# A queue of deferred work gets borders: the steps of a layer norm's chain dealt one to a pair of weight blocks, and no flush before the pointwise product

## The chip, the cores and the metric

The kernel runs on one core of one Trainium2 chip. TensorE (PE in the profile) multiplies matrices, VectorE (DVE) and ScalarE (ACT) work on tiles in the on-chip memory, GpSimd (POOL) takes a few small steps, and SyncE (SP) issues nearly all transfers. Each engine works through its own list of instructions in a fixed order and waits for the others by semaphores. The metric is the device time of one execution in microseconds (us); less is better.

## The reference, cut to what matters

One layer of a streaming encoder on a sequence of 256 rows and a width of 4096, all in float32:

```python
xn = rms_norm(h, norm_in_g[i])
proj = xn @ w_in[i]                       # 4096 x 14336
q, k, v, z_a, a_c, g_c, z_c = jnp.split(proj, ...)          # seven times 2048 columns
y_a = rms_norm(chunked_attention(q, k, v, rel_table[i]), attn_out_g[i]) * jax.nn.silu(z_a)
# the convolution module, 2048 channels
u = a_c * jax.nn.sigmoid(g_c)
u = causal_depthwise_conv(u, w_dw) + b_dw                    # 31 taps
u = jax.nn.silu(layer_norm(u, ln_g, ln_b))
y_c = rms_norm(u @ w_pw + b_pw, conv_out_g[i]) * jax.nn.silu(z_c)
h = h + jnp.concatenate([y_a, y_c], axis=-1) @ w_out[i]
gate = jax.nn.sigmoid(rms_norm(h, ple_norm_g[i]) @ w_ple_gate[i] + b_ple_gate[i])
h = h + gate * (p[i] @ w_ple[i])
return rms_norm(h, final_g)
```

## The kernel before, in words

Every large product takes its operands as a rounded high part and the rest as a low part, and adds three products: high by high, low by high, high by low. So each weight block that a transfer brings (`wt`, 128 rows by 2 x 512 columns) is split on the spot: ScalarE casts it to `wh` (L218), VectorE subtracts to get `wl` (L219), and TensorE reads both (L386). The tiles `wh` and `wl` have three buffers each, so a cast waits until TensorE has done with the block three before.

`mixed_product` makes two output groups of 512 columns at once. It goes through 16 "pairs" of weight blocks in an order written by hand (`early` and `valued`, for instance). A plain pair is two blocks of 12 products each. A pair with a star is a "seven": it is done with 21 products in place of 24, for which VectorE must add up weights first (`ua`, `ub`, L442 to L447) and both engines must split four tiles. At the last seven `on_helpers` collects the sums of the helper banks (`acc_P..`) into the tiles `z`; after the last pair the results in the banks `acc` are added to `z` (L510).

Work that is not urgent waits in a queue, `later`: a list of small functions. After each pair, `deal(n)` calls `fill(n)`, which pops n functions and so writes their instructions into the program at that place, behind that pair's weight cast (`behind_casts`); it then writes one step of the attention from a second list, `heads`. The numbers n stand in tables, one for each pair: `early_fills`, or a tuple at the call. A scheduler then fixes the order on each engine; the place at which a function is written says where it may stand at the earliest, more than where it will stand.

The change concerns two such products that follow each other, and what comes after. The first (`q, vs[2] = blocks(...)`, order `early`) makes the fourth group of queries and the third of values; here the last 56 taps of the convolution are dealt out and the layer norm begins. The second (`k, vs[3] = blocks(...)`, order `valued`) makes the last keys and values; here the rest of the layer norm is dealt out. Then the pointwise product with `w_pw` begins, which reads the layer norm's result as the tiles `uS` (named `big_t`).

The layer norm works on four tiles `cv` of 128 x 1024, one for 512 channels. Its chain is: `total` (sums over the tiles), `fold`, `mean` (a product on TensorE), then `center` 16 times (L766) and `square` 4 times (L770, L774), `fold`, `variance` (two small products L780, then a power on GpSimd, tile `r_ln`), `diagonals` (two VectorE steps, L789), `spread` (products L798, then ScalarE writes `rs`, L749), then `swish` 16 times (a multiply by `rs` on VectorE, L803, and Silu on ScalarE, L804, behind a table load), and `split` 16 times (a cast on ScalarE, L814, and a subtraction on VectorE, L815, into `uS`). Between the steps of the chain stand empty functions, `rest`, four at a time, which use up places of the tables. What is left in the queue when the two products end is written at once by `fill(len(later))` ahead of the pointwise product: 20 functions, four `swish` and 16 `split`.

`late_pool`, called at the last seven of the second product, closes a pool and opens another, `more`, in which `uS` lies; no `split` can be written earlier.

Of the kernel before, what the change touches and what calls it, by code (L numbers as in the profile page):

```python
# [17 lines left out]
NB = 512  # L18
# [7 lines left out]
def hybrid_block(  # L26
# [24 lines left out]
    _, T, D = x.shape  # L51
# [34 lines left out]
    def tmp_psum():  # L86
        return ps_tmp.tile([P, 512], F32, tag="tmp", name="tmp_ps")
# [6 lines left out]
    o_q, o_k, o_v, o_za = 0, AW, 2 * AW, 3 * AW  # L94
# [41 lines left out]
    def rsqrt(dst, src, n):  # L136

        nc.vector.tensor_scalar(dst, src, 1.0 / n, EPS, ALU.mult, ALU.add)
        nc.gpsimd.tensor_tensor(dst, dst, mhalf[:, : dst.shape[1]], ALU.pow)
# [9 lines left out]
    def big_tile(pool=None):  # L149
        return (pool or big).tile([P, 4, 2, T], F32R, tag="big", name="big_t")  # L150
# [29 lines left out]
    later = deque()  # L180
# [3 lines left out]
    def behind_casts():  # L184
        return tc.issue_after(last_cast[0].ins) if last_cast else nullcontext()

    def fill(n):
        with behind_casts():
            for _ in range(min(n, len(later))):
                later.popleft()()  # L190

    heads = deque()
# [1 line left out]
    def deal(n):  # L194
        fill(n)
        if heads:
            with behind_casts():
                heads.popleft()()
# [129 lines left out]
    def units(text):  # L328

        return [(int(u.rstrip("*")), u.endswith("*")) for u in text.split()]  # L330
# [4 lines left out]
    early = units("1 3 5 7 0* 9 2* 11 4* 13 6* 15 8 10 12 14")  # L335

    valued = units("1 3 5 7 8 0* 9 2* 10 4* 11 6* 12 13 14 15")

    early_fills = (4, 6, 7, 1, 5, 1, 5, 1, 5, 1, 2, 4, 6, 6, 6, 4)
# [149 lines left out]
    def sum_tiles(**kw):  # L489

        kw = kw or dict(tag="stage")
        t = [spool.tile([P, NH, NB], F32, name="z", **kw) for _ in range(2)]
        return t, [[t[j][:, h] for j in range(2)] for h in range(NH)]

    def scaled_pair(w, col, apart, order, r, fills, home={}, then=lambda: None, **kw):

        t, z = [], []

        def on_helpers(helper):
            for dst, src in zip((t, z), sum_tiles(**home)):  # L500
                dst.extend(src)
            then()
            nc.scalar.activation(z[0][0], helper["P1"], AF.Identity, scale=r[:, :1])
            helper_sums(helper, z)
            for h, j in QUARTERS[1:]:
                nc.scalar.activation(z[h][j], z[h][j], AF.Identity, scale=r[:, h : h + 1])

        c = mixed_product(w, col, xT, xS, order, on_helpers, fills=fills, apart=apart, **kw)
        for h, j in QUARTERS:
            stt(  # L510
                z[h][j], c[h][j], r[:, h : h + 1], z[h][j],
                ALU.mult, ALU.subtract if j else ALU.add,
            )
        return t
# [222 lines left out]
    def layer_norm_swish():  # L737

        add = nc.vector.tensor_tensor
        st = {}  # L740

        def fold(s):
            add(s[:, :2, :], s[:, :2, :], s[:, 2:, :], ALU.add)
            add(s[:, 0, :], s[:, 0, :], s[:, 1, :], ALU.add)
            return s[:, 0, :]

        def stat(key, m, scale=1.0):
            st[key] = cpool.tile([P, T], F32, tag="ln_stat", name=key)
            nc.scalar.activation(st[key], m, AF.Identity, scale=scale)  # L749

        def mean(s):

            m = tmp_psum()
            nc.tensor.matmul(m[:, :T], mean_w, s, start=True, stop=True)
            stat("mu", m[:, :T])

        def total(c):
            if c == 0:
                st["s"] = hd_tile("lnsum")
                add(st["s"], conv[0], conv[1], ALU.add)  # L760
            elif c > 1:
                add(st["s"], st["s"], conv[c], ALU.add)

        def center(c, i):
            cv = conv[c]
            nc.vector.tensor_tensor(cv[:, i, :], cv[:, i, :], st["mu"], ALU.subtract)  # L766

        def square(c):
            s = hd_tile("sq")
            nc.scalar.activation(s, conv[c], AF.Square)  # L770
            if c == 0:
                st["q"] = s
            else:
                add(st["q"], st["q"], s, ALU.add)  # L774

        def variance(s):

            m = tmp_psum()
            for h in range(NH):
                nc.tensor.matmul(  # L780
                    m[:, h : h + 1], s[:, h * P : (h + 1) * P], mean_w[:, :1],
                    start=True, stop=True,
                )
            st["r"] = cpool.tile([P, NH], F32, name="r_ln")
            rsqrt(st["r"], m[:, :NH], 1)

        def diagonals(s):
            for h in range(NH):
                nc.vector.tensor_scalar(  # L789
                    s[:, h * P : (h + 1) * P], ident, st["r"][:, h : h + 1], None, ALU.mult  # L790
                )

        def spread(s):

            m = tmp_psum()
            for h in range(NH):
                d = s[:, h * P : (h + 1) * P]
                nc.tensor.matmul(m[:, h * P : (h + 1) * P], mean_w, d, start=True, stop=True)  # L798
            stat("rs", m[:, :T], float(CW))

        def swish(c, i):
            cv, b = conv[c], 4 * c + i
            nc.vector.tensor_tensor(cv[:, i, :], cv[:, i, :], st["rs"], ALU.mult)  # L803
            nc.scalar.activation(  # L804
                cv[:, i, :], cv[:, i, :], AF.Silu,
                scale=ln_g[:, b : b + 1], bias=ln_b[:, b : b + 1],
            )

        def split(c, i):
            if i == 0:  # L810
                assert more is not None
                uS.append(big_tile(more))
            hi, lo = uS[c][:, i, 0, :], uS[c][:, i, 1, :]
            nc.scalar.copy(hi, conv[c][:, i, :])  # L814
            nc.vector.tensor_tensor(lo, conv[c][:, i, :], hi.bitcast(F32), ALU.subtract)  # L815

        n = len(conv)
        rest = [lambda: None] * 4
        later.extend(partial(total, c) for c in range(n))
        later.append(lambda: fold(st["s"]))  # L820
        later.extend(rest)
        later.append(lambda: mean(st["s"][:, 0, :]))
        later.extend(rest)
        for c in range(n):
            later.extend(partial(center, c, i) for i in range(4))
            later.append(partial(square, c))
        later.append(lambda: fold(st["q"]))
        later.extend(rest)
        later.append(lambda: variance(st["q"][:, 0, :]))
        later.extend(rest)  # L830
        later.append(lambda: diagonals(st["s"][:, 0, :]))
        later.extend(rest)
        later.append(lambda: spread(st["s"][:, 0, :]))
        later.extend(rest)
        for c in range(n):
            later.extend(partial(swish, c, i) for i in range(4))
        for c in range(n):
            later.extend(partial(split, c, i) for i in range(4))
# [84 lines left out]
    qs, ks, vs, biases = {}, {}, {}, {}  # L923

    def hd_tile(name):
        return spool.tile([P, GH, T], F32, tag="hd", name=name, bufs=5)

    def load_bias(g):
        bias = biases[g] = hd_tile("bias")
        span = 2 * MAXR + 1  # L930
        nc.sync.dma_start(
            bias,
            bass.AP(
                tensor=rel_table.tensor,
                offset=rel_table.offset + g * GH * span + MAXR + P - (T - 1),
                ap=[[1, P], [span, GH], [1, T]],
            ),
        )
        nc.gpsimd.memset(bias[: P // 2, :, : P // 2], NEG)

    def queries(g, q):
        qs[g] = act.tile([P, GH, T], F32, tag="act", name="qT")
        to_heads(q, qs[g])
# [5 lines left out]
    def blocks(cols, order, fills, **kw):  # L949
        return scaled_pair(w_in0, cols[0], cols[1] - cols[0], order, r_x, fills, **kw)  # L950
# [9 lines left out]
    def late_pool():  # L960
# [18 lines left out]
    keys(2, early_fills)  # L979
    layer_norm_swish()  # L980
    load_bias(2)
    q, vs[2] = blocks((o_q + 3 * NB, o_v + 2 * NB), early, (4,))
    queries(3, q)
    attention(2)
    k, vs[3] = blocks(
        (o_k + 3 * NB, o_v + 3 * NB), valued, (5, 5, 4, 5, 4, 2, 3, 2, 3, 2, 3, 4, 4, 4, 4, 4),
        then=late_pool,
    )
    keyed(3, k)
# [8 lines left out]
        )  # L998
        return t

    fill(len(later))

    point = units("0 1 2 3 4 5 6 7")
    y_c = []
# [175 lines left out]
    _, z = sum_tiles()  # L1180
# [60 lines left out]
    def sum_of(h, at):  # L1241
        s = end[:, 0, h : h + 1]
        pin(nc.vector.tensor_reduce(s, ssq_f[:, h, :at], AX.X, ALU.add))
        return s
# [45 lines left out]
    s = sum_of(1, n_f + 1)  # L1290
# [35 lines left out]
```

## Time and profile before

| | us |
|---|---|
| median of three timed runs | 2039.97 |
| the three runs | 2035.58, 2039.97, 2040.53 |
| the profiled execution | 2035.71 |
| its span, from the first to the last instruction | 2033.9 |
| TensorE busy in the span | 2015.2 |
| VectorE busy | 1912.3 |
| ScalarE busy | 1184.6 |
| TensorE's mean granted clock, share of full | 0.998 |

The four executions known fall in two pairs, 2035.6 and 2035.7, 2040.0 and 2040.5; their mean is 2037.9. The profiled one belongs to the lower pair. A busy share of an engine is the time in which one of its instructions ran, over the span; TensorE's products overlap each other, so the pace at which they start says more about it than how long one takes.

### The profile page before, as it was taken

To read this page: it belongs to the slowest core of one execution; us is meant where nothing else is said; L and a number is where in the kernel's file an instruction comes from. 1 tells how busy PE (TensorE), PEld (TensorE's weight loads), DVE (VectorE), ACT (ScalarE), POOL (GpSimd) and SP (SyncE) were. 2 spreads that over 40 slices of the span, in tenths; PEclk is the share of its full clock that TensorE was granted. 3 is DMA by queue.
4 is the path that set the end of the run, shared out by engine and by line. 5 is a ranking of instruction groups with operands and counts; after the bars stand their busy time and mean duration, and the time that the engine had idled before them with its cause. 6 is when DMAs were issued, how large, how long until landed. Compare 5 with 4: busy or idle time off the path is not lost.

```text
span 2033.9 us, 25980 instructions
## 1 busy us (share of the span) xinstructions
PE 2015.2 (99%) x9094; PEld 1661.5 (82%) x9094; DVE 1912.3 (94%) x2728; ACT 1184.6 (58%) x1530; POOL 7.7 (0%) x19
## 2 busy tenths in 40 slices
PE   9999999999999999999999999999999999999997
PEld 7888888888888888878888888888888888888876
DVE  7999999989999998986899999999999999999998
ACT  7655545555455544675566566676565666665555
POOL 0000000000000000000000000000000000000000
PEclk9999999999999999999999999999999999999999
DMA  8666666566665666555666666676666656666765
GB/s 288 194 196 203 202 196 197 176 196 192 205 205 166 196 199 195 175 186 186 190 217 202 197 210 210 220 232 206 208 199 212 209 187 207 199 223 204 234 208 179
DMA packets 157756, 412.28 MB, mean 203 GB/s; under 512 B 12974, under 2 KB 16190, under 8 KB 157626
## 3 DMA queue, kind: packets, MB, share of 16 engines
q1 hardware_dynamic: 156976, 409.80, 63.4%
q8 instruction: 71, 1.16, 0.2%
q10 hardware_dynamic: 650, 0.84, 0.1%
q14 instruction: 59, 0.48, 0.1%
HBM read 406.39 MB, written 4.19 MB: 202 GB/s over the span
## 4 chain that ended last, share of the span: by engine, by line
PE 53%; DVE 1%; issue 1%; ACT 0%; DMA 0%; POOLq 0%; POOL 0%; ACTq 0%; DVEq 0%
PE acc L386 40%; PE acc_P L386 12%; PE acc L233 1%; PE tmp_ps L170 1%; DVE wl L219 0%; DMA wt<-in_w_ple_dram 0%; DMA wt<-in_w_in_dram 0%; DVE big_t L815 0%; ACT wh L218 0%; ACT uh L218 0%; DVE ul L219 0%; ACT hc L1256 0%; DVE z L1196 0%; PE tmp_ps L891 0%; DVE z L1232 0%
## 5 line engine op out<-in xcount | busy, mean ns | idle before, releaser
L386 PE MATMUL acc<-wh,big_t 128*128 128x512 f32 x4252 | 1312.3, 391 | 0.8 <-DVE wh L577 0.5
L218 ACT CAST wh<-wt 128x1024 fp32r<-128x1024 f32 (+1 forms) x737 | 712.8, 978 | 562.0 <-PE acc L386 409.9
L386 PEld LDWEIGHTS acc<-wh,big_t 128*128 128x128 f32 x4252 | 795.4, 188 | 166.8 <-ACT big_t L156 1.3
L219 DVE TENSOR_TENSOR wl<-wt,wh 128x1024 fp32r<-128x1024 f32 (+1 forms) x737 | 823.6, 1130 | 49.8 <-ACT wh L218 46.7
L386 PE MATMUL acc<-wl,big_t 128*128 128x512 f32 x2126 | 819.7, 391 | 2.3 <-DVE wl L219 2.1
L386 PEld LDWEIGHTS acc<-wl,big_t 128*128 128x128 f32 x2126 | 398.8, 188 | 87.5 <-DVE wl L219 4.5
L696 DVE SCALAR_TENSOR_TENSOR cv<-uT,dw,cv 128x249 f32<-128x249 f32 (+22 forms) x480 | 209.4, 467 | 0.6
L218 ACT CAST uh<-ub 128x1024 fp32r<-128x1024 f32 x126 | 132.5, 1051 | 119.1 <-DVE ub L447 100.9
L218 ACT CAST uh<-ua 128x1024 fp32r<-128x1024 f32 x126 | 132.7, 1053 | 84.3 <-DVE ua L443 78.8
L386 PE MATMUL acc_P<-uh,big_t 128*128 128x512 f32 x528 | 161.9, 392 | 0.0
L219 DVE TENSOR_TENSOR ul<-ub,uh 128x1024 fp32r<-128x1024 f32 x126 | 153.9, 1221 | 7.3 <-ACT uh L218 6.7
L219 DVE TENSOR_TENSOR ul<-ua,uh 128x1024 fp32r<-128x1024 f32 x126 | 153.9, 1221 | 0.4 <-ACT uh L218 0.2
L386 PEld LDWEIGHTS acc_P<-uh,big_t 128*128 128x128 f32 x528 | 98.0, 188 | 23.0 <-ACT uh L218 3.5
L442 DVE TENSOR_TENSOR ua<-wt 128x512 f32<-128x512 f32 x126 | 86.7, 688 | 23.1 <-DMA wt<-in_w_in_dram 14.6
L386 PE MATMUL acc_P<-ul,big_t 128*128 128x512 f32 x264 | 101.6, 393 | 0.0
L443 DVE TENSOR_TENSOR ua<-wt 128x512 f32<-128x512 f32 x126 | 86.5, 686 | 1.9 <-DMA wt<-in_w_in_dram 1.8
L447 DVE TENSOR_TENSOR ub<-ub,wt 128x512 f32<-128x512 f32 x126 | 86.6, 687 | 0.6
L446 DVE TENSOR_TENSOR ub<-ua,wt 128x512 f32<-128x512 f32 x126 | 86.5, 687 | 0.3
L386 PE MATMUL acc_P<-wh,big_t 128*128 128x512 f32 x252 | 78.0, 390 | 0.0
L386 PE MATMUL acc<-uh,big_t 128*128 128x512 f32 x252 | 78.0, 390 | 0.0
L386 PE MATMUL acc_P<-uh,comb_t 128*128 128x512 f32 x228 | 70.3, 391 | 0.1
L386 PEld LDWEIGHTS acc_P<-ul,big_t 128*128 128x128 f32 x264 | 49.4, 188 | 13.1 <-DVE ul L219 2.8
(212 smaller groups left out, 1310.3 us busy)
## 6 DMA issues: line engine op xcount, KB each, us to landing
wt<-in_w_in_dram SPq DMA_DIRECT2D x447, 512.0 KB, 4.1
wt<-in_w_out_dram SPq DMA_DIRECT2D x128, 512.0 KB, 4.2
wt<-in_w_ple_gate_dram SPq DMA_DIRECT2D x128, 512.0 KB, 4.1
wt<-in_w_pw_dram SPq DMA_DIRECT2D x32, 512.0 KB, 4.7
hc<-in_x_dram SPq DMA_DIRECT2D x8, 512.0 KB, 5.8
wt<-in_w_ple_dram SPq DMA_DIRECT2D x8, 512.0 KB, 4.4
xin<-in_x_dram SPq DMA_DIRECT2D x7, 512.0 KB, 7.9
out_dram<-hc SPq DMA_DIRECT2D x12, 256.0 KB, 2.5
```

The lines of the kernel that those rows point to most:

```text
L170: nc.tensor.transpose(pt[:, i * T + h * P : i * T + (h + 1) * P], src[:, h, b] if len(src.shape) == 4 else src[:, h, b * P : (b + 1) * P], ...
L218: nc.scalar.copy(wh[:, :kc, :], wt[:, :kc, :]),
L219: nc.vector.tensor_tensor(wl[:, :kc, :], wt[:, :kc, :], wh[:, :kc, :].bitcast(F32), ALU.subtract),
L233: nc.tensor.matmul(acc, a, b[:, k, :], start=kb == 0 and kind == 0, stop=kb == kblocks - 1 and kind == 2,)
L386: nc.tensor.matmul(banks[name], a, b, start=name not in begun, stop=final and ends[name] == n and kind == 2 and not (left and name in "P2 ...
L442: plus(ua[:, 0], w0[:, 0], w0[:, 1])
L443: plus(ua[:, 1], w0[:, 1], w1[:, 1])
L446: plus(ub[:, 0], ua[:, 0], w1[:, 1])
L447: plus(ub[:, 1], ub[:, 0], w1[:, 0])
L696: nc.vector.scalar_tensor_tensor(cv[:, i, PAD - k :], uT[:, i, : T + k - PAD], dw[:, b, k : k + 1], cv[:, i, PAD - k :], ALU.mult, ALU.add,)
```

## The change

A border, `None`, may stand in the queue. `fill` stops at a border, and the next `fill` of at least one removes it and goes on. The empty functions are gone; a border stands behind each of the six chain steps `fold`, `mean`, `fold`, `variance`, `diagonals` and `spread`, so that two of these steps are never written after the same pair. The first product takes the table `early_fills` in place of four functions after each pair, the second has a new table, and the queue is empty when the second product ends, so the flush is replaced by an assertion.

```diff
     def fill(n):
+
         with behind_casts():
-            for _ in range(min(n, len(later))):
+            if n and later and later[0] is None:
+                later.popleft()
+            for _ in range(n):
+                if not later or later[0] is None:
+                    break
                 later.popleft()()
...
-        rest = [lambda: None] * 4
         later.extend(partial(total, c) for c in range(n))
-        later.append(lambda: fold(st["s"]))
-        later.extend(rest)
-        later.append(lambda: mean(st["s"][:, 0, :]))
-        later.extend(rest)
+        later.extend((lambda: fold(st["s"]), None, lambda: mean(st["s"][:, 0, :]), None))
         for c in range(n):
             later.extend(partial(center, c, i) for i in range(4))
             later.append(partial(square, c))
-        later.append(lambda: fold(st["q"]))
-        later.extend(rest)
-        later.append(lambda: variance(st["q"][:, 0, :]))
-        later.extend(rest)
-        later.append(lambda: diagonals(st["s"][:, 0, :]))
-        later.extend(rest)
-        later.append(lambda: spread(st["s"][:, 0, :]))
-        later.extend(rest)
+        later.extend((lambda: fold(st["q"]), None, lambda: variance(st["q"][:, 0, :]), None))
+        later.extend((lambda: diagonals(st["s"][:, 0, :]), None, lambda: spread(st["s"][:, 0, :]), None))
...
-    q, vs[2] = blocks((o_q + 3 * NB, o_v + 2 * NB), early, (4,))
+    q, vs[2] = blocks((o_q + 3 * NB, o_v + 2 * NB), early, early_fills)
...
-        (o_k + 3 * NB, o_v + 3 * NB), valued, (5, 5, 4, 5, 4, 2, 3, 2, 3, 2, 3, 4, 4, 4, 4, 4),
+        (o_k + 3 * NB, o_v + 3 * NB), valued, (1, 5, 5, 5, 6, 1, 1, 1, 6, 3, 7, 3, 5, 5, 3, 0),
...
-    fill(len(later))
+    assert not later
```

By these tables, in the second product, `swish` is now written after the 9th to 11th pair, where it was after the 14th to 16th and in the flush, and `split` after the 12th to 15th pair, where all of it was in the flush.

What the scheduler makes of it is seen in three places. The names are those of the text above; line numbers behind the queue's function are five higher in the kernel after the change. In the second product, ScalarE, from the scaling factor `rs` on, before:

```order
L749 ACTIVATE rs<-tmp_ps 128x256
L506 ACTIVATE z<-z,r_x 128x512
L218 CAST wh<-wt 128x1024
L506 ACTIVATE z<-z,r_x 128x512 x2
L804 ACT_TABLE_LOAD
L804 ACTIVATE cv<-cv,prm 128x256 x4
L218 CAST wh<-wt 128x1024 x2
L804 ACTIVATE cv<-cv,prm 128x256 x4
L218 CAST wh<-wt 128x1024 x2
L804 ACTIVATE cv<-cv,prm 128x256 x8
L814 CAST big_t<-cv 128x256 x16
L218 CAST wh<-wt 128x1024 x4
```

The same stretch of ScalarE after the change:

```order
L754 ACTIVATE rs<-tmp_ps 128x256
L223 CAST wh<-wt 128x1024
L809 ACT_TABLE_LOAD
L809 ACTIVATE cv<-cv,prm 128x256 x16
L511 ACTIVATE z<-z,r_x 128x512 x3
L819 CAST big_t<-cv 128x256 x8
L223 CAST wh<-wt 128x1024
L819 CAST big_t<-cv 128x256 x5
L223 CAST wh<-wt 128x1024 x2
L819 CAST big_t<-cv 128x256 x3
L223 CAST wh<-wt 128x1024 x7
```

The weight casts that stood between the Silus now stand behind all of them: 16 Silus, the three scalings of `z` and eight casts of `split` follow each other with no `wh` between, while the run of `split` casts ahead of the pointwise product's first weights is gone.

At the border between the second product and the pointwise product, TensorE before (`kT` are the keys, `tmp_ps` the scores, `wh_7929` and `wl_7930` the pointwise product's first weights):

```order
L851 MATMUL tmp_ps_7868<-ident_103,z_7666 128x128 x4
L868 MATMUL tmp_ps_7961<-kT_7861,qT_7024 128x128
L869 MATMUL tmp_ps_7961<-kT_7861,qT_7024 128x256
L386 MATMUL acc00_7921<-wh_7929,big_t_7882 128x512 x2
L386 MATMUL acc10_7923<-wh_7929,big_t_7882 128x512 x2
L386 MATMUL acc01_7922<-wh_7929,big_t_7882 128x512 x2
L386 MATMUL acc11_7924<-wh_7929,big_t_7882 128x512 x2
L868 MATMUL tmp_ps_7973<-kT_7861,qT_7024 128x128
L869 MATMUL tmp_ps_7973<-kT_7861,qT_7024 128x256
L386 MATMUL acc00_7921<-wl_7930,big_t_7882 128x512
```

TensorE at the same border after the change:

```order
L846 MATMUL tmp_ps_7912<-ident_103,z_7703 128x128 x4
L391 MATMUL acc00_7921<-wh_7929,big_t_7721 128x512 x2
L391 MATMUL acc00_7921<-wl_7930,big_t_7721 128x512
L391 MATMUL acc10_7923<-wh_7929,big_t_7721 128x512 x2
L391 MATMUL acc10_7923<-wl_7930,big_t_7721 128x512
L391 MATMUL acc01_7922<-wh_7929,big_t_7721 128x512 x2
L391 MATMUL acc01_7922<-wl_7930,big_t_7721 128x512
L391 MATMUL acc11_7924<-wh_7929,big_t_7721 128x512 x2
L391 MATMUL acc11_7924<-wl_7930,big_t_7721 128x512
L391 MATMUL acc00_7921<-wh_7945,big_t_7721 128x512 x2
```

The first products with `kT` have moved behind the first two blocks of pointwise weights, and the low part `wl_7930` is read in the usual place, right behind the high part.

In the first seven of the second product (`ua` and `ub` are its sums of weights), VectorE before:

```order
L774 TENSOR_TENSOR sq<-sq 128x1024
L219 TENSOR_TENSOR wl<-wt,wh 128x512
L219 TENSOR_TENSOR ul<-ua,uh 128x1024
L446 TENSOR_TENSOR ub<-ua,wt 128x512
L766 TENSOR_TENSOR cv<-cv,mu 128x256
L447 TENSOR_TENSOR ub<-ub,wt 128x512
L766 TENSOR_TENSOR cv<-cv,mu 128x256
L442 TENSOR_TENSOR ua<-wt 128x512
L443 TENSOR_TENSOR ua<-wt 128x512
L219 TENSOR_TENSOR wl<-wt,wh 128x1024
L219 TENSOR_TENSOR ul<-ub,uh 128x1024
```

VectorE in the same seven after the change:

```order
L779 TENSOR_TENSOR sq<-sq 128x1024
L451 TENSOR_TENSOR ub<-ua,wt 128x512
L748 TENSOR_TENSOR sq<-sq 128x512
L224 TENSOR_TENSOR ul<-ua,uh 128x1024
L749 TENSOR_TENSOR sq<-sq 128x256
L224 TENSOR_TENSOR wl<-wt,wh 128x1024
L452 TENSOR_TENSOR ub<-ub,wt 128x512
L447 TENSOR_TENSOR ua<-wt 128x512
L224 TENSOR_TENSOR wl<-wt,wh 128x1024
L224 TENSOR_TENSOR ul<-ub,uh 128x1024
```

The sum of squares is complete one seven earlier: its last addition and its fold (`sq`, 128x512 and 128x256) now stand in this seven, between the sums of weights.

## The prediction

> **What bounds the kernel now.** I read the page's busy times first, then the waits of TensorE, then busy times by stage around the layer norm, then the order of time at the stage that stands out.
>
> ```profile
> span 2033.9 us, 25980 instructions
> PE 2015.2 (99%) x9094; PEld 1661.5 (82%) x9094; DVE 1912.3 (94%) x2728; ACT 1184.6 (58%) x1530; POOL 7.7 (0%) x19
> PE acc L386 <- DVE wl L219: 2.1, 1, 2.1
> PE tmp_ps L868 <- DVE kT L856: 0.8, 1, 0.8
> DVE lnsum L789 <- POOL r_ln L139: 0.8, 1, 0.8
> 808.00:836.00 28.00, 28.00 (x147) 23.86 (x145) 26.74 (x57) 19.48 (x42) 0.00 (x0) 1.00 0.53 158
> 836.00:868.00 32.00, 31.87 (x141) 26.08 (x140) 29.04 (x33) 18.48 (x21) 0.31 (x1) 1.00 0.65 214
> 868.00:894.40 26.40, 26.40 (x121) 21.68 (x120) 20.62 (x39) 22.54 (x41) 0.70 (x1) 1.00 0.60 179
> 894.40:903.40 9.00, 6.04 (x31) 4.46 (x30) 9.00 (x21) 5.91 (x12) 0.00 (x0) 1.00 0.20 61
> ```
>
> TensorE is the bound: 2015.2 of 2033.9 us. The change moves no product into or out of its list, so all that can change is its idle time, 18.7 us in the whole span. The third to fifth lines are waits (how long in all, how often, longest). The last four lines are stretches from start to end of the second product and the border behind it (length, then busy time of PE, its weight loads, DVE, ACT, POOL, then TensorE's clock and the transfers): TensorE never waits in the second product, and is idle for 9.00 - 6.04 = 2.96 us at the border. That is all the change can win there, 0.15%.
>
> ```profile
> 891.29 5.00 ACT L814 CAST big_t<-cv 128x256 fp32r<-128x256 f32 x16
> 894.58 1.03 PE L851 MATMUL tmp_ps<-ident,z 128*128 128x128 f32 x8
> 896.19 2.94 ACT L218 CAST wh<-wt 128x1024 fp32r<-128x1024 f32 x3
> 896.44 0.49 PE L868 MATMUL tmp_ps<-kT,qT 128*128 128x128 f32 x2 [0.82 <-DVE kT L856]
> 896.90 4.09 DVE L815 TENSOR_TENSOR big_t<-cv,big_t 128x256 fp32r<-128x256 f32 x12
> 900.92 2.34 DVE L219 TENSOR_TENSOR wl<-wt,wh 128x1024 fp32r<-128x1024 f32 x2
> 902.19 1.20 PE L386 MATMUL acc<-wl,big_t 128*128 128x512 f32 x4 [2.13 <-DVE wl L219]
> ```
>
> Here (start, length, engine, line) the flush is seen: 16 `split` casts hold ScalarE until 896.19, the last 12 subtractions hold VectorE from 896.90, and `wl` starts only at 900.92. TensorE waits 2.13 us for it, and 0.82 us for the keys `kT`.
>
> **Part 1, the flush removed: -2.95 us.** Both waits, 2.13 + 0.82, go. No `split` stands ahead of `wl`, and the products with `kT` now stand behind two pointwise blocks, 5.4 us of work, while the copies into `kT` need under 2. Ends: -3.0 and -1.5, if a wait of half the size takes their place.
>
> **Part 2, the run on ScalarE: +5.9 us.** Its prices, with TensorE's pace beside them:
>
> ```profile
> 870.92 1.05 ACT L218 CAST wh<-wt 128x1024 fp32r<-128x1024 f32 x1 [1.03 <-PE acc L386]
> 870.95 0.62 PE L386 MATMUL acc_P<-uh,big_t 128*128 128x512 f32 x2
> 872.33 0.61 PE L798 MATMUL tmp_ps<-lnsum,mean_w 128*128 128x128 f32 x4
> 876.51 1.33 ACT L506 ACTIVATE z<-z,r_x 128x512 f32<-128x512 f32 x2
> 877.82 4.44 DVE L803 TENSOR_TENSOR cv<-cv,rs 128x256 f32<-128x256 f32 x13
> 877.84 1.28 ACT L804 ACT_TABLE_LOAD   x1
> 878.25 0.62 PE L386 MATMUL acc<-wh,big_t 128*128 128x512 f32 x2
> 879.14 2.08 ACT L804 ACTIVATE cv<-cv,prm 128x256 f32<-128x256 f32 x4
> 880.97 0.61 PE L386 MATMUL acc<-wh,big_t 128*128 128x512 f32 x2
> 881.12 1.99 ACT L218 CAST wh<-wt 128x1024 fp32r<-128x1024 f32 x2
> 887.35 4.04 ACT L804 ACTIVATE cv<-cv,prm 128x256 f32<-128x256 f32 x8
> ```
>
> The order shows the run between two weight casts. From the start of the one to the end of the other: the cast 0.95 (two take 1.99, the second 1.05 of it), the table load 1.30 (877.84 to 879.14), 16 Silus 7.9 (eight take 891.29 - 887.35 = 3.94), three scalings of `z` 1.9 (two take 1.33), eight `split` casts 2.45 (16 take 896.19 - 891.29 = 4.90), the next weight cast 1.05. Sum 15.55 us.
>
> How long can TensorE go on? The cast ahead of the run takes the buffer of the last seven's second block. In the trace that cast starts at 870.92, as TensorE gives the buffer back, and TensorE still has the rest of the seven to do, 870.95 to 872.33 = 1.4 us. Then come three plain blocks with `wh` made, at 2.72 us each (878.25 to 880.97 are four of the groups of three products, a block): 8.15. So TensorE runs dry after 9.6 us and waits 15.55 - 9.6 = 5.9 us. The number of buffers and the order are fixed, so both sums run from the same event; ends 5.2 and 6.5. The 16 multiplies on VectorE cost nothing more: they come at 0.34 us each (13 take 4.44), faster than the Silus at 0.49 that wait for them; the sums of `z` behind them are done before ScalarE gets to the scalings, 10 us into its run; and a `wl` that they delay only moves the time at which TensorE starts to wait for the same `wh`. When the `wh` comes, its `wl` still takes VectorE about 1.2 us, and TensorE has two products to do until it reads it: 0.35 us more at half pace, 0.75 at full; I take 0.35.
>
> In the kernel before, the longest stretch without a weight cast is 887.4 to 896.2, 8.8 us, where it is 15.55 - 0.95 - 1.05 = 13.55 after; and there TensorE had the transposes, the scores and the wait for `kT` in hand beside its blocks.
>
> **Part 3, the clock: +2.5 us.** A wait of 6 us is longer than any in this trace, so what the clock does is bounded by its ends.
>
> ```profile
> 1.18 2.32 PE L125 MATMUL tmp_ps<-idle 128*128 128x512 bf16 x5 [1.18 <-DVE ssq_f L1134]
> 8.57 1.08 PE L386 MATMUL acc<-wl,big_t 128*128 128x512 f32 x4
> 901.00:902.20 1.20, 0.01 (x1) 0.01 (x1) 1.20 (x2) 0.00 (x0) 0.00 (x0) 1.00 0.00 0
> 2020.12 1.24 PE L374 MATMUL part<-big_t 128*128 128x256 f32 x9
> 2021.40:2023.90 2.50, 0.00 (x0) 0.00 (x0) 1.92 (x6) 1.49 (x6) 0.00 (x0) 1.00 1.03 383
> 2024.00:2030.00 6.00, 0.00 (x0) 0.00 (x0) 2.45 (x7) 2.56 (x4) 0.93 (x1) 0.50 0.55 204
> ```
>
> The last product ends at 2021.4, and the granted clock goes from 1.00 to 0.50 about 2.6 us later. The 2.13 us at the border left it at 1.00. At the kernel's start five products take 2.32 us, 0.43 each, and only at 8.57 are they at 0.23: TensorE comes up to pace about 5.5 us after its first product. So a wait of 6 us should halve the clock, and the products behind it run at half pace for some 5 us, which loses 2.5. Ends: 0 (no drop, the border's row) and 2.75 (5.5 us, the start's row); I take the value near the start's row, as the wait is over twice the 2.6 us.
>
> [...]
>
> **Part 4, smaller waits: +0.9 us.** In both kernels TensorE's list has `variance` and `spread` in the last seven, though they are written three or four pairs earlier after the change. Before, 12 products lie between them, 869.5 to 872.3; after, four, 0.9 us. In between, VectorE and GpSimd make `r_ln` and the diagonals, where VectorE waits 0.8 us for GpSimd and the whole takes about 1.3. That is +0.4 (0 to 0.8).
>
> In the first seven the fold of the squares has come in:
>
> ```profile
> 828.50 1.22 DVE L774 TENSOR_TENSOR sq<-sq 128x1024 f32<-128x1024 f32 x1
> 835.02 0.69 DVE L443 TENSOR_TENSOR ua<-wt 128x512 f32<-128x512 f32 x1 [0.96 <-DMA wt<-in_w_in_dram]
> 836.77 1.22 DVE L219 TENSOR_TENSOR ul<-ub,uh 128x1024 fp32r<-128x1024 f32 x1
> 839.62 0.39 PE L386 MATMUL acc_P<-ul,comb_t 128*128 128x512 f32 x1
> 841.91 0.69 DVE L743 TENSOR_TENSOR sq<-sq 128x512 f32<-128x512 f32 x1
> 843.65 0.42 DVE L744 TENSOR_TENSOR sq<-sq 128x256 f32<-128x256 f32 x1
> ```
>
> Ahead of `ul<-ub` VectorE now has one more addition of squares (1.1), the two folds (0.6 + 0.3) and, net of what moves behind it, about 0.6 of weight splits: 2.6 us. It was ready at 838.0 and read at 839.6, 1.6 us of slack, and the 0.96 us for which VectorE waited for a transfer is gone from its place. That covers it but for chance; the table of the first product deals most at its end, which makes VectorE somewhat later here. I take +0.5, ends 0 and 2.
>
> **Parts at nothing.** The borders cost no instruction. The 24 empty functions and the six borders issue none. In the first product the same 61 functions are dealt, only elsewhere, under a TensorE that is busy throughout. SP's list has one load of `bias` two weight loads earlier and one of `b_pw` one later; the transfers fill a fifth of the border's stretch, 0.20. POOL's list is the same.
>
> **The sum.** -2.95 + 5.9 + 0.35 + 2.5 + 0.4 + 0.5 = +6.7 us, 0.33%. Against the profiled execution's own 2035.71 that is 2042.4. The four executions known lie at 2035.6 and 2035.7 and at 2040.0 and 2040.5, without a cause that the page shows; I take their mean 2037.9 as the base: 2037.9 + 6.7 = 2044.6. Ends of the sum: -3.0 + 5.2 + 0.35 = +2.5 and -1.5 + 6.5 + 0.75 + 2.75 + 0.8 + 2 = +11.3.
>
> **Rivals.**
> The clock holds. Then the wait costs 5.9 + 0.75, and the sum is -2.95 + 6.65 + 0.9 = +4.6: 2042.5. For it, the border's 2.13 us left the clock alone; against it, the drop after 2.6 us at the end.
>
> The run on ScalarE is covered, and the flush's removal is what counts. It decides when the run is shorter than the 9.6 us that TensorE has in hand, or exceeds it by less than 2 us. For it: before, 8.8 us passed without a weight cast and cost nothing. Against: the sum of rows is 15.55. With the wait gone, the clock stays: -2.95 + 0.9 = -2.05, 2035.9; not slower.
>
> VectorE is the bound in the first seven and the seven behind it, at the upper end of part 4 and once more in the next: +2 more, 2046.6 to 2047. For it, VectorE is busy 26.74 of 28.00 us there; against it, TensorE lost 0.13 us in the next 32.
>
> [...]
>
> That the change doesn't do what it says is true in part already: in the order the chain's steps stand where they stood, and only what follows has moved. This is in the sum.
>
> **Chances.** The run is not covered and the clock drops, my forecast: 0.77, of which 0.5 lies over 0.3%. The clock holds: 0.11. The run is covered: 0.06. VectorE adds to it: 0.06. About 0.3%, 6.1 us, is what a measurement of this kernel can tell from no change. So slower 0.5 + 0.06 = 0.56; within 0.3%: 0.27 + 0.11 + 0.03 = 0.41; faster by more, the covered run on a lucky base, 0.03. The range: from 2037, the covered run's -2 to -3 on the median of 2040, to 2050, the forecast's upper part on the higher pair: 2040.2 + 10.
>
> **What would show it.** In the profile after: no wait of TensorE for `wl` or `kT` at the border; one wait of TensorE for `wh<-` ScalarE's cast of some 6 us in the second product's 14th pair, behind 16 Silus in a row; a granted clock of 0.50 for 2 to 6 us around it, and starts of products 0.43 us apart behind it. If that wait is 3 us or less, part 2 is wrong; if the clock stays at 1.00, part 3; if TensorE waits in the first seven for `ul` over 1 us, part 4.

## The result, and the profile after

| | before | after |
|---|---|---|
| median of 22 runs each, us | 2037.53 | 2041.96 |
| lowest and highest, us | 2033.69, 2040.71 | 2040.04, 2043.68 |
| profiled execution, us | 2035.71 | 2042.02 |

The ratio is 1.0021, with a 95% interval of 1.0014 to 1.0027: the changed kernel is slower by 2.8 to 5.5 us.

The page's head after the change, and TensorE's only two waits from the second product to the border (how long in all, how often, longest):

```profile
span 2040.2 us, 25987 instructions
PE 2016.9 (99%) x9094; PEld 1662.2 (81%) x9094; DVE 1913.8 (94%) x2728; ACT 1184.1 (58%) x1530; POOL 8.3 (0%) x19
PE acc L391 <- ACT wh L223: 5.9, 1, 5.9
PE tmp_ps L803 <- DVE lnsum L794: 0.4, 1, 0.4
```

The waits for `wl` and `kT` at the border are gone, and one of 5.9 us for `wh` has come. The stretches of the second product, the border in the last (columns as before: length, busy time of PE, its weight loads, DVE, ACT, POOL, then clock and transfers):

```profile
836.00:868.00 32.00, 32.00 (x143) 26.39 (x142) 28.64 (x34) 19.20 (x21) 0.00 (x0) 1.00 0.63 198
868.00:894.40 26.40, 20.04 (x82) 15.10 (x81) 21.56 (x46) 23.07 (x45) 0.70 (x1) 0.87 0.37 117
894.40:910.00 15.60, 15.60 (x76) 13.01 (x75) 10.46 (x12) 5.54 (x6) 0.00 (x0) 1.00 0.62 211
```

All is lost in the second row: TensorE is idle for 6.36 of 26.40 us, at a mean clock of 0.87. ScalarE and TensorE in order of time there:

```profile
872.00 1.04 ACT L223 CAST wh<-wt 128x1024 fp32r<-128x1024 f32 x1
873.07 1.28 ACT L809 ACT_TABLE_LOAD   x1
874.36 7.99 ACT L809 ACTIVATE cv<-cv,prm 128x256 f32<-128x256 f32 x16
882.26 1.93 ACT L511 ACTIVATE z<-z,r_x 128x512 f32<-128x512 f32 x3
884.10 2.53 ACT L819 CAST big_t<-cv 128x256 fp32r<-128x256 f32 x8
886.53 1.04 ACT L223 CAST wh<-wt 128x1024 fp32r<-128x1024 f32 x1
...
881.33 0.39 PE L391 MATMUL acc<-wl,big_t 128*128 128x512 f32 x1
887.63 1.22 PE L391 MATMUL acc<-wh,big_t 128*128 128x512 f32 x2 [5.91 <-ACT wh L223]
889.48 1.05 PE L391 MATMUL acc<-wh,big_t 128*128 128x512 f32 x2
891.60 0.39 PE L391 MATMUL acc<-wl,big_t 128*128 128x512 f32 x1
```

From the start of one weight cast, 872.00, to the end of the next, 887.57, 15.57 us pass, and between the two ScalarE is busy with Silus, scalings and `split` casts; TensorE has used up its last `wh` by 881.72. The clock, cut where it changes:

```profile
881.34:884.75 3.41, 0.38 (x2) 0.00 (x0) 0.28 (x2) 3.41 (x9) 0.00 (x0) 1.00 0.30 115
884.75:888.16 3.41, 0.53 (x1) 0.50 (x2) 3.09 (x9) 3.41 (x11) 0.00 (x0) 0.50 0.00 0
888.16:891.57 3.41, 3.37 (x8) 2.15 (x7) 3.41 (x8) 3.41 (x9) 0.00 (x0) 0.50 0.37 129
891.57:894.98 3.41, 3.41 (x16) 2.82 (x15) 3.35 (x6) 1.41 (x3) 0.00 (x0) 1.00 0.62 189
```

It is at half for 6.83 us, of which 3.9 lie behind the wait; there products start some 0.43 us apart, where they start 0.23 apart at full clock, from 891.60 on.

A more exact account lays the starts of TensorE's products side by side, since its list has the same 9094 products in every kernel, in places in another order (the unread ones of two experiments are left out). The rows give how much later the product of that number starts than in the trace of before; the column "3701 to 4101" is what the second product and the border cost, the last the difference of the medians in the runs made together.

| kernel | 3701 (before: 817.1) | 3931 (866.4) | 4021 (886.2) | 4101 (906.6) | 3701 to 4101 | medians |
|---|---|---|---|---|---|---|
| after | 0.35 | -0.05 | 8.83 | 5.12 | **+4.8** | +4.4 |
| after, again | 2.08 | 1.64 | 11.30 | 7.59 | **+5.5** | +5.1 |
| `e_bytile` | 0.38 | -0.06 | 1.24 | -2.44 | **-2.8** | -2.8 |
| `e_late` | 1.00 | 0.57 | 1.16 | 2.72 | **+1.7** | +2.1 |
| `e_warm` | 1.69 | 1.29 | 8.17 | 4.46 | **+2.8** | +3.7 |
| `e_warm`, again | 0.07 | -0.35 | 6.55 | 2.84 | **+2.8** | +2.5 |
| `e_splitlate` | 1.84 | 1.45 | 9.07 | 5.95 | **+4.1** | +3.0 |
| `e_bank` | 1.21 | 1.35 | 2.18 | -0.87 | **-2.1** | -2.1 |
| `e_bwarm` | -0.73 | -1.09 | -1.10 | -1.09 | **-0.4** | -2.0 |

So of the 6.3 us between the two spans 4.8 come from here; the rest lies elsewhere in the program, in pieces of 0.1 to 1 us that are others in each trace (the column of product 3701 shows up to 2.1 us ahead of the place).

### The profile page after: what moved, and what is told of

Same layout as the page of the kernel before. It is cut to its first block, busy times and chain, and to the rows that moved or that the text cites. A ratio compares the mean times of both kernels' runs of the same rounds, so it can differ in the third digit from the quotient of the medians.

```text
span 2040.2 us, 25987 instructions
## 1 busy us (share of the span) xinstructions
PE 2016.9 (99%) x9094; PEld 1662.2 (81%) x9094; DVE 1913.8 (94%) x2728; ACT 1184.1 (58%) x1530; POOL 8.3 (0%) x19
## 3 DMA queue, kind: packets, MB, share of 16 engines
q8 instruction: 71, 1.16, 0.3%
## 4 chain that ended last, share of the span: by engine, by line
PE 53%; DVE 1%; issue 1%; DMA 0%; ACT 0%; POOLq 0%; POOL 0%; ACTq 0%; DVEq 0%
PE acc L391 40%; PE acc_P L391 11%; PE acc L238 1%; PE tmp_ps L170 1%; DVE wl L224 0%; DMA wt<-in_w_out_dram 0%; PE acc L379 0%; DMA wt<-in_w_in_dram 0%; DVE ul L224 0%; ACT wh L223 0%; PE tmp_ps L864 0%; PE pacc L238 0%; DVE ua L448 0%; ACT hc L1251 0%; PE tmp_ps L886 0%
```

## The experiments

**The same queue, dealt by tile (`e_bytile`).** Silus and splits of one tile follow each other, eight functions after each of the last four pairs; so the Silus are also written later, after the 13th to 16th pair, where it was the 9th to 11th. Theory A of the expectations is that the run on ScalarE starves TensorE.

```diff
         for c in range(n):
             later.extend(partial(swish, c, i) for i in range(4))
-        for c in range(n):
             later.extend(partial(split, c, i) for i in range(4))
...
-        (o_k + 3 * NB, o_v + 3 * NB), valued, (1, 5, 5, 5, 6, 1, 1, 1, 6, 3, 7, 3, 5, 5, 3, 0),
+        (o_k + 3 * NB, o_v + 3 * NB), valued, (1, 5, 5, 5, 6, 1, 1, 1, 0, 0, 0, 0, 8, 8, 8, 8),
```

> The queue hands out the four Silus of a tile and at once its four splits, one tile after each of the last four pairs; borders, both tables up to there and the missing flush stay as in the changed kernel. Theory A (the 15.57 us run on ScalarE between two weight casts starves TensorE for 5.91 us, and the halved clock behind it costs some 2 us more): ScalarE's longest stretch without a weight cast falls to about 8 us, below the 9.6 us TensorE has in hand; no wait for wh over 1 us, clock 1.00 to the end, no wait at the border; the time is 5.9 + 2 = about 8 us under the changed kernel less the disturbance of its own, and 2 to 3 us under the kernel before (ratio to before 0.9985 to 0.999). Rival B (the loss comes from what is dealt earlier, in the first product and the first sevens, which this kernel keeps): the wait goes but the time stays 2 to 4 us above before.

Measured: 2033.59 us (11 runs) against 2036.37 (33 runs), ratio 0.9987 (0.9978 to 0.9996). ScalarE, and TensorE's only wait from the second product to the border:

```profile
873.06 1.28 ACT L809 ACT_TABLE_LOAD   x1
874.35 0.60 ACT L809 ACTIVATE cv<-cv,prm 128x256 f32<-128x256 f32 x1
...
879.40 1.05 ACT L223 CAST wh<-wt 128x1024 fp32r<-128x1024 f32 x1
880.36 2.07 ACT L809 ACTIVATE cv<-cv,prm 128x256 f32<-128x256 f32 x4
882.33 1.31 ACT L819 CAST big_t<-cv 128x256 fp32r<-128x256 f32 x4
883.55 1.99 ACT L223 CAST wh<-wt 128x1024 fp32r<-128x1024 f32 x2
PE tmp_ps L803 <- DVE lnsum L794: 0.4, 1, 0.4
```

The first part, from the cast at 871.99 to the end of the one at 879.40, takes 8.46 us and fits into what TensorE has in hand; the parts behind it are shorter. The wait for `wh` is gone, the border has none, and the kernel is faster than both. Borders, early steps and the missing flush are all kept, so none of these is the loss. Rival B falls. This run does not separate the dealing by tile from the later place of the Silus.

**The late part dealt late (`e_late`).** The new tables as far as the second product's eighth pair, then Silus after the last three pairs, and the flush.

```diff
-        (o_k + 3 * NB, o_v + 3 * NB), valued, (1, 5, 5, 5, 6, 1, 1, 1, 6, 3, 7, 3, 5, 5, 3, 0),
+        (o_k + 3 * NB, o_v + 3 * NB), valued, (1, 5, 5, 5, 6, 1, 1, 1, 0, 0, 0, 0, 0, 4, 4, 4),
...
-    assert not later
+    fill(len(later))
```

> Borders and the new tables of the first product and of the second one's first eight pairs stay; Silus are dealt after the last three pairs, the rest is written at once at the end, as in the kernel before. Theory A: no long run between weight casts inside the product, so no wait for wh, clock up; the waits at the border come back (wl about 2, kT about 0.8); the time is that of the kernel before within 1.5 us (ratio 0.9995 to 1.0007). Rival B (the early part of the queue carries the loss): 3 to 5 us above before, as the changed kernel (ratio 1.002).

Measured: 2038.47 us (11 runs) against 2036.37, ratio 1.0006 (0.9997 to 1.0014): the time does not tell it from before, and the upper end of the interval, 2.9 us, comes close to the 3 of rival B. The ratio lies in the forecast range; the medians are 2.1 us apart, where 1.5 was the most expected. The trace tells more: from product 3931 to 4021 it differs from before by 0.6, the wait ahead of `spread`, and all else comes at the border, where the two waits are back, 2.1 and 0.8 us, and the clock falls behind them, which it had not in the trace of before. The two waits and the windows of the clock, `e_late` first, then the windows of before:

```profile
PE acc L391 <- DVE wl L224: 2.1, 1, 2.1
PE tmp_ps L863 <- DVE kT L851: 0.8, 1, 0.8
900.23:903.64 3.41, 1.28 (x7) 0.84 (x6) 3.41 (x8) 0.34 (x2) 0.00 (x0) 1.00 0.00 0
903.64:907.05 3.41, 3.41 (x9) 2.64 (x9) 3.41 (x10) 3.38 (x9) 0.00 (x0) 0.50 0.69 173
```

```profile
897.55:900.96 3.41, 2.51 (x12) 1.76 (x11) 3.41 (x12) 1.59 (x2) 0.00 (x0) 1.00 0.26 90
900.96:904.37 3.41, 2.18 (x9) 1.80 (x10) 3.41 (x8) 2.14 (x2) 0.00 (x0) 1.00 0.31 89
```

The pieces of one clock that the traces record between changes last 2017.28 us in before, 877.23, 6.83 and 1140.05 us after the change, which is 591, 257, 2 and 334 times 3.413 us; the one at half in `e_late` lasts 3.41 us, from 903.64 to 907.05. Stretches of 3.41 us, counted from a recorded change, are called windows here; where no change is recorded, their edges are an estimate from these multiples. In `e_late` the window ahead of the fall holds the wait of 2.13 us and was busy for 1.28 us, and the next was granted half; before, counted back from the change at 2023.94, an edge at 900.96 cuts the same wait into windows busy for 2.51 and 2.18 us, and the clock stayed up. Of `e_late`'s executions, three show a mean clock of 0.998 and take 2035.4 us on average, eight show 0.997 and take 2039.1.

**No idle time at the border of before (`e_bwarm`).** If the phase of these windows makes the scatter of the kernel before, then work for TensorE at its border must end it.

```diff
+    last_transpose_kT = [None]
...
-                    nc.tensor.transpose(
+                    last_transpose_kT[0] = nc.tensor.transpose(
...
+    bank = tmp_psum()
+    with tc.issue_after(last_transpose_kT[0].ins):
+        for _ in range(11):
+            nc.tensor.matmul(
+                bank, xT[7][:, 0, 0, :P], xT[7][:, 0].rearrange("q a t -> q (a t)"),
+                start=True, stop=True,
+            )
     fill(len(later))
```

> The kernel before with 11 products of 128x512 added, whose result nobody reads, on TensorE at the border, right behind the transposes of the keys, where it waits 0.82 and 2.13 us; 11 at 0.23 us are 2.5 us, so they take up the second wait or the first and part of it. The mean clocks of before's executions are 0.998 in 15 and 0.997 in 18 of 33 on record, with mean times of 2035.9 and 2036.9. Theory F (in some executions the clock falls at the border's waits and costs up to 2 us; this is the scatter of the kernel before): clock 0.998 in all executions, the scatter narrower, the slowest of them at most 2 us over the median, the median 0 to 1.2 us under before. Rival G (the scatter has another cause): 0.997 in about half of the executions still, scatter unchanged, median equal or up to 1.5 us higher by the products that do not fit into the wait.

Measured: 2035.49 us, lowest and highest 2033.86 and 2036.36 (11 runs), against 2037.46, 2034.36 and 2040.89 (28 runs), ratio 0.9993 (0.9984 to 1.0002). The clock is 0.998 in all 11 runs.

```profile
894.27 2.78 PE L1006 MATMUL tmp_ps<-big_t 128*128 128x512 f32 x11
901.09 1.20 PE L386 MATMUL acc<-wl,big_t 128*128 128x512 f32 x4 [0.92 <-DVE wl L219]
```

The products took the place of the waits and won no time against the trace of before (-1.09 at product 3931, -1.09 at 4101), and yet no execution is above 2036.4. Over both sets of runs, before took 2035.9 us on average in 27 executions at a clock of 0.998 and 2037.5 in 34 at 0.997. Rival G falls, and theory F holds for the scatter: with the gap filled, the high executions are gone. Its size was missed, since the median is 2.0 us under before, where 0 to 1.2 was expected. Nor does the dip explain all of the 4.4 us between the two pairs of times at which the prediction stopped: by estimate, one window at a clock of 0.50 costs at most half of its 3.41 us, 1.7, and the two groups of executions lie 1.6 apart on average and overlap. The rest stays open.

**The wait filled (`e_warm`), twice, the second time beside the changed kernel.** 24 unread products stand on TensorE right ahead of the block that waits.

```diff
-        left=(), begin=None,
+        left=(), begin=None, between={},
...
                     add_plain(n, k, *parts_of(wts[k], 2)[0])
+                    if (n, k) in between:
+                        bank = tmp_psum()
+                        with tc.issue_after(made[-1].ins):
+                            for _ in range(between[n, k]):
+                                nc.tensor.matmul(
+                                    bank, lhs[7][:, 0, 0, :P],
+                                    lhs[7][:, 0].rearrange("q a t -> q (a t)"),
+                                    start=True, stop=True,
+                                )
...
-        then=late_pool,
+        then=late_pool, between={(13, 0): 24},
```

> The changed kernel with 24 products of 128x512 added, whose result nobody reads, on TensorE right ahead of the block for which it waits 5.91 us; 24 at 0.23 us are 5.4 us, so they fill the wait and add nothing to it. Theory A with the clock: the granted clock stays 1.00, products behind the wait start 0.23 us apart at once, and 2.0 to 2.2 us come back (ratio to before about 1.001, 2 us under the changed kernel). Rival C (the clock's dip costs nothing, since VectorE's low parts or ScalarE's casts limit TensorE there anyway): clock 1.00, but the time of the changed kernel within 0.5 us.

> The changed kernel with the 24 unread products of 128x512 in TensorE's wait, again, now beside the changed kernel on the same chip. Between the last product of the last seven's fold and the pointwise product the first trace of it loses 3.2 us against before, where the changed kernel loses 5.2 and the two have the same rows else. Theory A with the clock: median 1.5 to 2.5 us under the changed kernel of this call, mean clock 0.997 to 0.998. Rival C (the clock's dip costs nothing): the medians of the two agree within 0.7 us.

> The changed kernel once more, unaltered, so that the two kernels below it on this chip can be set beside it. Both theories: about 4.4 us over before (ratio 1.0014 to 1.0027), mean granted clock 0.996, one wait of 5.9 us for wh.

Measured: ratios 1.0016 (1.0007 to 1.0025) and 1.0013 (1.0005 to 1.0022) for `e_warm`, 1.0029 (1.0017 to 1.0040) for the changed kernel; medians of the second set of runs 2039.97 us (11 runs) and 2042.51 (6 runs), of the first 2040.09 (11 runs). The lines are from the first trace of `e_warm`:

```profile
882.90 5.60 PE L439 MATMUL tmp_ps<-big_t 128*128 128x512 f32 x24
888.98 1.66 PE L391 MATMUL acc<-wh,big_t 128*128 128x512 f32 x6 [0.48 <-ACT wh L223]
882.90:888.50 5.60, 5.60 (x25) 4.32 (x23) 2.64 (x8) 5.60 (x14) 0.00 (x0) 1.00 0.14 53
888.50:892.00 3.50, 3.02 (x13) 2.52 (x14) 3.17 (x8) 3.50 (x8) 0.00 (x0) 1.00 0.13 44
```

`wh` comes no earlier, but the six products behind the wait take 1.66 us at full pace, and 2.5 us are won by the medians, 2.0 and 2.7 by the table. The clock's dip costs time, and rival C falls. The two intervals of the second set overlap a little (1.0017 to 1.0022), so it is the traces, which agree in both sets, that carry this.

**A shorter run (`e_splitlate`).** The splits wait for the flush; Silus as changed.

```diff
-        (o_k + 3 * NB, o_v + 3 * NB), valued, (1, 5, 5, 5, 6, 1, 1, 1, 6, 3, 7, 3, 5, 5, 3, 0),
+        (o_k + 3 * NB, o_v + 3 * NB), valued, (1, 5, 5, 5, 6, 1, 1, 1, 6, 3, 7, 0, 0, 0, 0, 0),
...
-    assert not later
+    fill(len(later))
```

> The changed kernel with the 16 splits left in the queue until the end and written at once there, as before; all else of the queue as changed. The order shows the run on ScalarE without its eight casts of split: 15.57 - 2.45 = 13.1 us, and 16 casts in a row after five more weight casts. Theory A (the wait is run less what TensorE has in hand, 9.7 us): one wait for wh of 3.4 us (3.0 to 3.9) in place of 5.9; the clock falls for one part of a window or not at all, at most half as long as in the changed kernel; a wait at the border of 0 to 2 us. Time 1.5 to 3.5 us under the changed kernel, 1 to 3 us over before. Rival E (the wait comes from the weights' transfers or VectorE's low parts and not from the length of the run): the wait stays at 5.9 or goes altogether.

Measured: 2040.46 us (11 runs), ratio 1.0016 (1.0008 to 1.0025), 2.1 us under the changed kernel.

```profile
886.68 1.22 PE L391 MATMUL acc<-wh,big_t 128*128 128x512 f32 x2 [3.46 <-ACT wh L223]
882.91:886.32 3.41, 0.31 (x2) 0.00 (x0) 0.00 (x0) 3.41 (x6) 0.00 (x0) 1.00 0.28 108
886.32:889.73 3.41, 3.01 (x6) 1.99 (x7) 3.07 (x3) 2.20 (x3) 0.00 (x0) 0.50 0.19 55
889.73:893.14 3.41, 3.41 (x9) 2.64 (x8) 0.42 (x1) 0.96 (x1) 0.00 (x0) 0.50 0.83 281
896.41 5.01 ACT L819 CAST big_t<-cv 128x256 fp32r<-128x256 f32 x16
PE acc L391 <- DVE wl L224: 0.3, 1, 0.3
```

From the start of one weight cast to the start of the next the run is 2.43 us shorter (873.50 to 885.60, where it was 872.00 to 886.53), and the wait is shorter by 5.91 - 3.46 = 2.45: the wait is the run less what TensorE has in hand, and rival E falls. The part on the clock missed: it is at half for two windows again, and 6.46 us of them now lie on products where it was 3.9, so the dip gives back part of what the shorter wait wins: by product 4021 only 1.3 of the 2.45 us are left. And 16 splits in a row stand ahead of the pointwise product again, with 0.3 us of waiting at the border: five weight casts now precede them. The flush of the splits alone is not what the border waits for; where Silus and splits both stood late, in before and in `e_late`, the two waits were there.

**The chain ahead of the sevens (`e_bank`).** Why `variance` stays in the last seven, though written long before it, is seen in the trace after; first the end of the sum of squares, then ScalarE's copy and `variance`:

```profile
834.79 0.42 DVE L749 TENSOR_TENSOR sq<-sq 128x256 f32<-128x256 f32 x1
868.95 0.52 PEld L785 LDWEIGHTS tmp_ps<-mean_w,sq 128*128 128x128 f32 x4 [0.41 <-ACT z L488]
868.95 0.60 PE L785 MATMUL tmp_ps<-mean_w,sq 128*128 128x1 f32 x4
```

Its input is ready at 835.2, and it waits 33.7 us, until ScalarE has copied a helper's sum to `z`: by the kernel it needs one of four banks of `tmp`, it is written right behind the first seven, and the sevens' helper sums hold all four banks from the first seven to the last. So the sevens are put two pairs later, and the table is shifted so that `variance`, `diagonals` and `spread` are written ahead of the first seven.

```diff
-    valued = units("1 3 5 7 8 0* 9 2* 10 4* 11 6* 12 13 14 15")
+    valued = units("1 3 5 7 8 9 10 0* 11 2* 12 4* 13 6* 14 15")
...
-        (o_k + 3 * NB, o_v + 3 * NB), valued, (1, 5, 5, 5, 6, 1, 1, 1, 6, 3, 7, 3, 5, 5, 3, 0),
+        (o_k + 3 * NB, o_v + 3 * NB), valued, (1, 7, 7, 7, 1, 1, 1, 0, 4, 2, 4, 2, 4, 4, 8, 4),
```

> The sevens of the second product stand later in its order (pairs 8, 10, 12, 14 in place of 6, 8, 10, 12), and the queue's numbers are shifted so that variance and spread are written before the first seven; no flush. Theory A with what the trace shows of the chain: variance waits in both kernels for one of the four banks of tmp, which the helper sums of the sevens hold until the last seven ends (ScalarE copies acc_P1 at 868.32 and variance starts at 868.95). Written before the sevens, variance and spread run ahead of them, some 25 us earlier against the product, and the Silus spread over several pairs: no run on ScalarE over 9 us, no wait for wh over 1 us, no border wait; 2 to 3 us under before. Rival D (it is the chain's own work on VectorE and GpSimd, not the bank, that holds variance until the last seven): variance and spread stay late, the Silus still bunch, and the wait of some 6 us stays or moves to the next pair: the time of the changed kernel or more.

Measured: 2034.28 us (11 runs), ratio 0.9986 (0.9978 to 0.9995).

```profile
836.98 0.50 PE L785 MATMUL tmp_ps<-mean_w,sq 128*128 128x1 f32 x4
849.24 0.38 ACT L754 ACTIVATE rs<-tmp_ps 128x256 f32<-128x256 f32 x1
PE acc L391 <- DVE wl L224: 1.0, 2, 0.7
```

`variance` now runs at 837.0, 3.3 us behind its input, and `rs` is there at 849.2 in place of 871.7; the Silus stand four and fewer at a time between weight casts, and no wait is over 0.7 us. Rival D falls. It and `e_bytile` gain about the same, 2.1 and 2.8 us, by two cures, moving the source or dividing the run.

## Why the prediction was right or wrong, point by point

The direction and the mechanism were right; the size was not. Slower by over 0.3% was the likeliest case, and 0.21% was measured, in the case of 0.41; with 22 runs each that is told from no change, though the prediction took 0.3% for the least that could be. The medians' +4.4 us lies next to the +4.6 of the rival in which the clock holds, but that is chance: the clock fell, and other terms were smaller. Between products 3701 and 4101 the sum of +6.7 us meets +4.8:

| term | predicted | measured there |
|---|---|---|
| flush removed | -2.95 | -3.7 |
| run on ScalarE | +5.9 | +6.1 |
| `wl` behind it, and the clock | +0.35 + 2.5 | +2.2 |
| ahead of `spread` | +0.4 | +0.6 |
| the sevens | +0.5 | -0.4 |

**Part 1.** Both waits went and no other came. The term was too small since it was read as idle time: in these traces a product takes 0.39 us and the next starts 0.23 behind it, so by estimate each wait costs some 0.16 us more than the idle time shows, and the first two products behind the wait for `wl` start 0.33 us apart. That makes some 3.5 of the 3.7 us. `e_splitlate` corrects the reason: 16 splits at once need not make the border wait.

**Part 2.** Held: a run of 15.57 us (15.55 forecast) and a wait of 5.91; `e_splitlate` moved both by 2.4. The table load took what the sum counts for it, 1.30 us: loads at 873.07 and 873.06, after the change and in `e_bytile`, are followed by Silus 1.29 us after their start.

**Part 3.** The clock fell, but the step that sized it, the 5.5 us read off the kernel's start, was wrong: it was at half for 6.83 us here, two windows (a little over the 2 to 6 us named as a sign), and 3.9 us of them lie behind the wait. The window ahead of the fall was busy for 0.38 us of 3.41 here, for 0.31 in `e_splitlate` and for 1.28 in `e_late`. "The border's row" as the lower end holds for the trace of before and not for that of `e_late`, though the wait for `wl` is 2.13 us in both.

**Part 4.** `spread` held. The 0.5 us for the first seven was too much: no product there waits.

```profile
838.60 1.22 DVE L224 TENSOR_TENSOR ul<-ub,uh 128x1024 fp32r<-128x1024 f32 x1
839.97 0.39 PE L391 MATMUL acc_P<-ul,comb_t 128*128 128x512 f32 x1
```

`ul<-ub` is ready at 839.8, 1.8 us later than before, and its product starts on time at 839.97: the slack of 1.6 us that the prediction counted, and 0.3 by which TensorE ran later here, were just enough, and the allowance for "chance" was not needed; the delay of 2.6 us that it feared was 1.8. The -0.4 is a wait of TensorE in a later seven of before (0.6 us for `wl`, at 858.96) that the trace after does not have. It is not shown to be the change's: `e_bwarm`, which is the kernel before up to the border, loses it too (from -0.73 at product 3701 to -1.09 at 3931). So the sevens cost about nothing, and against an execution of before without that wait the change would cost some 0.4 us more than +4.8.

**The base.** 2037.9 mixed two pairs of times. The medians of before were 2036.4 to 2037.5, so 0.4 us or more of the miss in 2044.6 is the base. The trace of before has no dip at the border. Of the 61 executions of before that the experiments were set against, 34 show a mean clock of 0.997 and 27 one of 0.998; that some of the 34 have a dip there is a reading, as they have no trace here. That the medians differ by less than the traces (+4.4 and +4.8) fits it, and doesn't show it.

**The rivals.** The clock did not hold, and by `e_warm` that is worth 2.0 to 2.7 us. The run was not covered. VectorE did not become the bound: TensorE is busy 32.00 of 32.00 us in the sevens. That the chain's steps stay where they stood was in the sum, without its cause, the banks of `tmp`.

## What to carry to other kernels

Work dealt out of a burst at the end can gather to a longer burst in the middle, if what it depends on comes late: look for the longest stretch without a cast on the engine that feeds TensorE, and hold it against what TensorE has in hand (here 9.6 us). Dealing by tile, all steps of one and then the next, divided the run here, as did starting the chain's last steps earlier. Ask of each step that stands late what resource it waits for, a bank as well as an input.

## What was not expected of the hardware

The same wait of 2.13 us was followed by a window at half clock in the trace of `e_late` and by full clock in that of before, and with 11 unread products in the gap all 11 executions of `e_bwarm` show 0.998. The mean clocks of 0.998 and 0.997 tell the two apart only roughly, since one window at half is worth 3.41 x 0.5 / 2034 = 0.0008: `e_bytile` and `e_bank`, with no wait at the border over 0.7 us, show 0.997 in one execution of 11 each.

While the clock was down, a window busy for 2.13 us of 3.41 (changed kernel, again, 888.06 to 891.47) or 3.01 (`e_splitlate`) was followed by another at half, and one busy for 3.37 (changed kernel) by full clock. For the fall, the end of `e_splitlate` gives one case more, in three windows in a row:

```profile
2026.38:2029.79 3.41, 1.77 (x15) 1.57 (x14) 2.77 (x8) 2.57 (x6) 0.00 (x0) 1.00 0.61 224
2029.79:2033.20 3.41, 0.00 (x0) 0.00 (x0) 2.96 (x9) 1.82 (x5) 0.93 (x1) 1.00 0.23 84
2033.20:2036.61 3.41, 0.00 (x0) 0.00 (x0) 0.36 (x1) 1.24 (x3) 0.00 (x0) 0.50 0.94 350
```

The window busy for 1.77 us is followed by one at full clock, and only the idle one by half. In the other traces, windows busy for 0.38 us (changed kernel) and 1.28 us (`e_late`) were followed by half clock. Whether busy time is what decides, for the fall or for the rise, these few cases do not show.
